# Output projection of a hybrid encoder layer: stores on another queue, loads issued two tiles ahead

## The chip, the core and the metric

The kernel runs on one core of a Trainium2 chip. TensorE (PE; PEld is its weight load) multiplies, VectorE (DVE), ScalarE (ACT) and GpSimd (POOL) do the rest, and SyncE (SP) and other engines issue DMA transfers between device memory and the on-chip buffers (SBUF; PSUM receives the matmuls). The metric is the device time of one execution in microseconds (us). SP's rows in the profile are DMA issues; a row with the engine name ACTq or POOLq is a DMA issued by that engine.

## The reference

One layer on 2048 tokens of width 1024, in float32. The normed input is projected; 8 heads of latent attention give 512 columns, a bidirectional S5 recurrence with GLU gives the other 512. Then, of the part that matters here:

```
mix = concat(rms_norm(attention) * g_a, rms_norm(s5) * g_s)     # 512 + 512 columns
h   = x + rms_norm(mix @ w_out) * g_post_mix                    # output projection
out = h + rms_norm(relu(rms_norm(h) @ w_up) ** 2 @ w_down) * g_post_mlp
```

## The kernel before, in words

The stages follow one another: input projection; attention head by head, with the S5 work in its gaps; the output projection, about 1583 to 1859 us of the profiled execution; the up projection of the MLP; the down projection. Each fp32 product is made of three matmuls of split halves (high and low part of each factor: `ah`/`al`, `sh`/`sl`, weights `woh`/`wol`).

Attention and S5 leave their results feature-major in DRAM: `AD` (attention, not yet divided by the softmax sums), `SD` (S5), and `RD2` (the reciprocals of the sums, two rows of heads per 128 features). The sums of the last head go to DRAM (`RD<-o`, L644), come back as `rr` (L647, GpSimd's queue), are inverted (L648) and stored (L649).

The output projection runs over 16 tiles of 128 tokens (`out_tile`). Per tile:

- `s_ops`: load `sr` from SD (L1116, one buffer), split into `sh`, `sl` (L125 on ScalarE, L126 on VectorE), square (L1109) and sum the blocks (`sq`, L1110).
- `a_ops`: load `ar` from AD (L1122, two buffers) and `rb` (L1126, two broadcast DMAs over 64 partitions each, one buffer), `ar` times `rb` on VectorE (L1128), then the same split, square and sum (`ah`, `al`, `aq`).
- `out_mm`: 24 matmuls on the S5 half and 24 on the attention half (`op`, L1182), into two PSUM banks each; two small products give the squared norms (`ss`), which VectorE copies to SBUF (`s2c`, L1203), and this frees their PSUM bank. GpSimd makes the two inverse norms (`rs_v`, `rs_r`, L131 and L132).
- ScalarE scales one half (`ot`, L1211), VectorE adds the other (`o`, L1212); ScalarE squares and sums (`jk`, L1216), VectorE scales by the norm and `gpo` (L1218) and adds the residual `xt` (L1219; loaded at L1196 in one buffer). `o` is stored to HD (L1220), squared once more (`jk`, L1225), and normed to `hn` (L1227).
- two tiles later (`hn_T`): 8 transposes (L1238), two copies to `hb` (L1243) and two stores to HTD (L1244), the feature-major input of the MLP.

Tile t is written with the attention factors of tile t+1 and the S5 factors of tile t+2 ahead of it. At tiles 10 and 11 a 1 MB load `traw` of HTD for the up projection is issued (L1273); from tile 9 on, factors of the first up weights (`raw`, `st`, L1264) are made between. All these DMAs but those of `rr` go through SP, in SP's program order: an issue that waits for a buffer or for a producer holds those behind it.

The order of each engine is not the program's: the Tile framework's scheduler places the instructions of each engine by a timeline model when the kernel is built, so a change in one place can move instructions elsewhere. PSUM has 8 banks, given out in turn.

Of the kernel before, what the change touches and what calls it, by code (L numbers as in the profile page):

```python
# [51 lines left out]
def hymba_layer_kernel(  # L52
# [75 lines left out]
    def rstd_of(ss, n, eps=EPS, rows=128):  # L128
        v = sm.tile([128, 1], F32, tag="rs_v", name="rs_v")
        r = sm.tile([128, 1], F32, tag="rs_r", name="rs_r")  # L130
        G.tensor_scalar(out=v[:rows], in0=ss, scalar1=1.0 / n, scalar2=eps, op0=ALU.mult, op1=ALU.add)  # L131
        G.tensor_tensor(out=r[:rows], in0=v[:rows], in1=mhalf[:rows], op=ALU.pow)  # L132
        return r
# [959 lines left out]
    def out_open():  # L1093
        ip = W["ip"] = ph.enter_context(pool("iO", 2, "right"))
        W["ep"] = ph.enter_context(pool("eO", 2, "right"))
        e1 = W["e1"] = ph.enter_context(pool("e1", 1, "right"))
        gpo = W["gpo"] = mk(e1, [128, D], "gpo")
        Y.dma_start(out=gpo, in_=g_post_mix[0].partition_broadcast(128))
        for t in range(2):
            W["s", t] = s_ops(t)  # L1100
            yield

    def halves(src, nm):
# [6 lines left out]
        V.reduce_sum(out=sq, in_=src.rearrange("p k c -> p c k"), axis=AX.X)  # L1110
        return h, l, sq

    def s_ops(t):
        cs = slice(t * 128, (t + 1) * 128)
        sr = W["ip"].tile([128, 4, 128], F32, tag="sr", name="sr", bufs=1)
        Y.dma_start(out=sr, in_=SD[:, cs].rearrange("(k p) c -> p k c", p=128))  # L1116
        return halves(sr, "s")

    def a_ops(t):
        cs = slice(t * 128, (t + 1) * 128)  # L1120
        ar = W["ip"].tile([128, 4, 128], F32, tag="ar", name="ar")
        Y.dma_start(out=ar, in_=AD[:, cs].rearrange("(k p) c -> p k c", p=128))  # L1122
        rb = W["ip"].tile([128, 4, 128], F32, tag="rb", name="rb", bufs=1)
        for b in range(2):
            src = RD2[b:b + 1, cs]
            Y.dma_start(out=rb[64 * b:64 * b + 64],  # L1126
                        in_=bass.AP(src.tensor, src.offset, [[0, 64], [2 * 2048, 4], [1, 128]]))
        V.tensor_tensor(out=ar, in0=ar, in1=rb, op=ALU.mult)  # L1128
        return halves(ar, "a")

# [57 lines left out]
        return sq, [out_mm(h, l, 4, half) for half in range(2)]  # L1188

    def out_tile(t, between):  # L1190
        if t + 1 < NT:
            W["a", t + 1] = a_ops(t + 1)
        if t + 2 < NT:
            W["s", t + 2] = s_ops(t + 2)
        xt = W["e1"].tile([128, D], F32, tag="xt", name="xt")
        Y.dma_start(out=xt, in_=xv[t // 8, t % 8])  # L1196
        sqs, ps = W.pop(("ps", t), None) or out_s(t)
        h, l, sqa = W.pop(("a", t))
        p = pa("ss")
        T.matmul(out=p[:, 0:2], lhsT=sqa, rhs=ones)  # L1200
        T.matmul(out=p[:, 2:4], lhsT=sqs, rhs=ones)
        s2 = sm.tile([128, 4], F32, tag="s2c", name="s2c")
        V.tensor_copy(s2, p[:, 0:4])  # L1203
        ra = rstd_of(s2[:, 0:1], 512)
        rb = rstd_of(s2[:, 2:3], 512, eps=4 * EPS)
        o = W["ep"].tile([128, D], F32, tag="o", name="o")
        for half in range(2):
            hs = slice(half * 512, (half + 1) * 512)
            p = out_mm(h, l, 0, half)
            tm = W["e1"].tile([128, 512], F32, tag="ot", name="ot")  # L1210
            S.activation(out=tm, in_=p, func=AF.Copy, scale=ra)  # L1211
            V.scalar_tensor_tensor(out=o[:, hs], in0=ps[half], scalar=rb, in1=tm, op0=ALU.mult, op1=ALU.add)  # L1212
        between()
        jk = W["e1"].tile([128, 512], F32, tag="ot", name="jk").bitcast(BF16)
        ss = sm.tile([128, 1], F32, tag="ss", name="ss")
        S.activation(out=jk, in_=o, func=AF.Square, accum_out=ss)  # L1216
        r = rstd_of(ss, D)
        V.scalar_tensor_tensor(out=o, in0=o, scalar=r, in1=W["gpo"], op0=ALU.mult, op1=ALU.mult)  # L1218
        V.tensor_tensor(out=o, in0=o, in1=xt, op=ALU.add)  # L1219
        Y.dma_start(out=HD[t], in_=o)  # L1220

        hn = wraw.tile([128, 8, 256], F32, tag="raw", name="raw")[:, 0:4].rearrange("p k c -> p (k c)") if t == NT - 1 else \
            W["e1"].tile([128, D], F32, tag="hn", name="hn", bufs=2)
        ss = sm.tile([128, 1], F32, tag="ss", name="ss")
        S.activation(out=jk, in_=o, func=AF.Square, accum_out=ss)  # L1225
        r = rstd_of(ss, D)
        V.scalar_tensor_tensor(out=hn, in0=o, scalar=r, in1=gpr, op0=ALU.mult, op1=ALU.mult)  # L1227
        return hn

    def hn_T(t, hn):  # L1230
# [10 lines left out]
        b = hn if t == NT - 1 else mk(tq, [128, D], "hb")  # L1241
        for a in range(2):
            S.copy(out=b[:, a * 512:(a + 1) * 512], in_=ps[a])  # L1243
            Y.dma_start(out=HTD[ct].rearrange("k p b c -> p k b c")[:, :, 2 * a + i // 4, cs],  # L1244
                        in_=b[:, a * 512:(a + 1) * 512].rearrange("p (k c) -> p k c", k=4))

    NP = FF // 256
# [23 lines left out]
    def s_load(ct, k):  # L1271
        RAW[ct, k] = raw = tst.tile([128, 4, 512], F32, tag="traw", name="traw")
        Y.dma_start(out=raw, in_=HTD[ct, k])  # L1273

    W["a", 0] = a_ops(0)
    for t in range(2):
        W["ps", t] = out_s(t)
# [291 lines left out]
```

## Time and profile before

| what | value |
|---|---|
| median of 3 runs | 3214.03 us (3213.02 to 3215.77) |
| the profiled execution, its own time | 3213.55 us |
| its span in the trace | 3211.7 us |
| mean granted TensorE clock | 0.973 |
| PE busy over the span | 3032.7 us, 94% |
| DVE, ACT, POOL busy | 1848.8, 1638.6, 1255.2 us |
| bytes on the hardware queue `q1` | 275.10 MB of 279.51 |
| output projection, first and last `s2c` | 1618.3 and 1835.6 us |

PE is busy 94% over the whole kernel, which says little of one stage. To read a stage, take the windows of time (how busy each engine is in it), then the waits in it (which engine waits, at which line, and for what), then the rows of one engine in order of time. A wait named "DMA ar<-AD" ends when that transfer has landed; the name of a tile stands without its buffer's number, so "RD" is `RD` or `RD2`.

### The profile page before, as it was taken

To read this page: it belongs to the slowest core of one execution; us is meant where nothing else is said; L and a number is where in the kernel's file an instruction comes from. 1 tells how busy PE (TensorE), PEld (TensorE's weight loads), DVE (VectorE), ACT (ScalarE), POOL (GpSimd) and SP (SyncE) were. 2 spreads that over 40 slices of the span, in tenths; PEclk is the share of its full clock that TensorE was granted. 3 is DMA by queue.
4 is the path that set the end of the run, shared out by engine and by line. 5 is a ranking of instruction groups with operands and counts; after the bars stand their busy time and mean duration, and the time that the engine had idled before them with its cause. 6 is when DMAs were issued, how large, how long until landed. Compare 5 with 4: busy or idle time off the path is not lost.

```text
span 3211.7 us, 42406 instructions
## 1 busy us (share of the span) xinstructions
PE 3032.7 (94%) x14455; PEld 2419.7 (75%) x14455; DVE 1848.8 (58%) x2893; ACT 1638.6 (51%) x3081; POOL 1255.2 (39%) x2363
## 2 busy tenths in 40 slices
PE   6999988989999999999879879999999999999998
PEld 6899956666777766678767658886888888888887
DVE  6333278767888876675356584448444234444447
ACT  4333356988777799974435445445445421111112
POOL 4222245775888876600032275447544000000002
PEclk8999989999999999999989989999999999999999
DMA  4232231211001022232246543333333422222215
GB/s 151 65 86 74 73 75 27 58 46 33 20 18 27 24 70 85 65 113 63 65 112 179 164 154 115 109 114 119 109 107 106 142 81 73 73 79 73 69 63 203
DMA packets 244377, 279.51 MB, mean 87 GB/s; under 512 B 35920, under 2 KB 180688, under 8 KB 243136
## 3 DMA queue, kind: packets, MB, share of 16 engines
q1 hardware_dynamic: 242112, 275.10, 28.1%
q8 instruction: 113, 1.85, 0.2%
q10 hardware_dynamic: 1792, 1.57, 0.2%
q14 instruction: 104, 0.85, 0.1%
q0 software_dynamic: 256, 0.14, 0.0%
HBM read 181.31 MB, written 95.36 MB: 86 GB/s over the span
## 4 chain that ended last, share of the span: by engine, by line
PE 57%; issue 6%; DVE 4%; ACT 4%; POOL 3%; DMA 2%; SPq 0%; POOLq 0%; DVEq 0%; ACTq 0%
PE dn L1514 20%; PE pE L1329 5%; PE pB L1329 5%; PE pA L1329 4%; PE s L619 3%; PE s L621 2%; PE s L620 2%; PE z L1079 2%; PE X L611 2%; PE pF L1329 2%; PE X L612 2%; PE X L613 2%; PE mxp L573 2%; POOL rs_r L132 1%; DMA rb<-RD 1%
## 5 line engine op out<-in xcount | busy, mean ns | idle before, releaser
L627 DVE TENSOR_TENSOR pl<-s,ph 128x512 fp32r<-128x512 f32 x512 | 350.2, 686 | 163.1 <-ACT s L626 157.0
L623 ACT ACTIVATE ph<-s 128x512 fp32r<-128x512 f32 (+1 forms) x544 | 323.4, 595 | 171.9 <-PE s L621 158.6
L1514 PE MATMUL dn<-dl,ah 128*128 128x512 f32 x1024 | 398.8, 389 | 0.0
L1514 PE MATMUL dn<-dh,ah 128*128 128x512 f32 x1024 | 398.8, 389 | 0.0
L1514 PE MATMUL dn<-dh,al 128*128 128x512 f32 x1024 | 398.7, 390 | 0.0
L574 DVE TENSOR_REDUCE mx<-mxp 128x1 f32<-128x512 f32 x512 | 343.0, 684 | 59.3 <-PE mxp L573 56.2
L125 ACT CAST ah<-mraw 128x512 fp32r<-128x512 f32 x128 | 79.5, 621 | 454.3 <-DMA mraw<-MD 273.8
L626 ACT ACTIVATE s<-s 128x512 f32<-128x512 f32 x512 | 304.1, 594 | 0.7
L1498 POOL TENSOR_TENSOR ss<-s2f 128x1 f32<-128x1 f32 x16 | 11.2, 699 | 702.2 <-ACT jk L1495 702.2
L1264 POOL TENSOR_TENSOR st<-raw 128x512 f32<-128x512 f32 x128 | 173.9, 1359 | 263.6 <-DVE al L126 263.5
L619 PE MATMUL s<-ql,kh 96*128 96x512 f32 (+1 forms) x544 | 226.9, 417 | 15.1 <-ACT ZS L937 4.9
L611 PE MATMUL X<-pl,vt 128*65 128x512 f32 x512 | 209.2, 409 | 29.8 <-DVE pl L627 27.9
L1519 DVE TENSOR_TENSOR acc<-dn,acc 128x512 f32<-128x512 f32 x224 | 153.0, 687 | 133.2 <-PE dn L1514 132.8
L1514 PEld LDWEIGHTS dn<-dl,ah 128*128 128x128 f32 x1024 | 192.4, 188 | 39.8
L1514 PEld LDWEIGHTS dn<-dh,al 128*128 128x128 f32 x1024 | 192.4, 188 | 39.7
L1514 PEld LDWEIGHTS dn<-dh,ah 128*128 128x128 f32 x1024 | 192.3, 188 | 39.7
L620 PE MATMUL s<-qh,kl 96*128 96x512 f32 (+1 forms) x544 | 218.3, 401 | 0.0
L621 PE MATMUL s<-qh,kh 97*128 97x512 f32 (+1 forms) x544 | 215.0, 401 | 0.7 <-DMA qh<-nm 0.7
L573 PE MATMUL mxp<-kh,qh 96*128 96x512 f32 x512 | 199.3, 411 | 13.2 <-DVE mx L574 5.2
L612 PE MATMUL X<-ph,vt 128*64 128x512 f32 x512 | 205.3, 401 | 0.0
L613 PE MATMUL X<-ph,vt 128*65 128x512 f32 x512 | 205.1, 401 | 0.0
L126 DVE TENSOR_TENSOR al<-mraw,ah 128x512 fp32r<-128x512 f32 x128 | 88.5, 691 | 197.8 <-ACT ah L125 188.2
(811 smaller groups left out, 7822.8 us busy)
## 6 DMA issues: line engine op xcount, KB each, us to landing
raw<-in_w_mlp_up_dram SPq DMA_DIRECT2D x32, 1024.0 KB
MD<-r SPq DMA_DIRECT2D x128, 256.0 KB
mraw<-MD SPq DMA_DIRECT2D x128, 256.0 KB
xt<-in_x_dram SPq DMA_DIRECT2D x32, 512.0 KB
raw<-in_w_mlp_down_dram SPq DMA_DIRECT2D x32, 512.0 KB
ug<-UD SPq DMA_DIRECT2D x32, 256.0 KB
HD<-o SPq DMA_DIRECT2D x16, 512.0 KB
traw<-HTD SPq DMA_DIRECT2D x8, 1024.0 KB
```

Of the source, the lines that this page charges most:

```text
L574: V.reduce_max(out=mxs[n][:, j, b:b + 1], in_=p, axis=AX.X)
L611: T.matmul(out=X[:65], lhsT=v[:, t, 0:65], rhs=pl_, start=(t == 0), stop=False)
L612: T.matmul(out=X[:64], lhsT=v[:, t, 65:129], rhs=ph_, start=False, stop=False)
L613: T.matmul(out=X[:65], lhsT=v[:, t, 0:65], rhs=ph_, start=False, stop=False)
L619: T.matmul(out=s[:m], lhsT=kh[0:96, cs], rhs=ql, start=True, stop=False)
L620: T.matmul(out=s[:m], lhsT=kl[:, cs], rhs=qh[0:96], start=False, stop=False)
L621: T.matmul(out=s[:m], lhsT=kh[:, cs], rhs=qh, start=False, stop=True)
L623: S.activation(out=ph_[:m], in_=s[:m], func=AF.Exp, scale=SCALE)
L626: S.activation(out=s, in_=s, func=AF.Exp, scale=SCALE)
L627: V.tensor_tensor(out=pl_, in0=s, in1=f(ph_), op=ALU.subtract)
L1329: T.matmul(out=p, lhsT=a[:, k], rhs=b, start=(first and k == 0 and j == 0), stop=(k == 3 and j == 2), skip_group_check=not first)
L1514: T.matmul(out=p, lhsT=a[:, ts_], rhs=c[:, hs], start=(q == 0 and w == 0), stop=(q == FB - 1 and w == 2))
```

## The change

In the output projection:

- The stores to HD (L1241 after) and HTD (L1260) are issued by ScalarE (`S.dma_start`) and no more by SP (`Y.dma_start`). HD stands behind the second `jk`.
- `loads(t)` issues `sr`, `xt`, `ar` and `rb` of a tile; `out_tile(t)` calls it for t+1 and t+2 at its head, so what isn't loaded yet is issued two tiles ahead.
- `sr`, `rb` have two buffers; `xt` moves to another pool (`tq`), also with two. `ar` had two and keeps them.
- The S5 factors of tile t+1 (they were those of t+2) are made in tile t.

```diff
--- before.py
+++ after.py
@@ -1097,6 +1097,7 @@
         gpo = W["gpo"] = mk(e1, [128, D], "gpo")
         Y.dma_start(out=gpo, in_=g_post_mix[0].partition_broadcast(128))
         for t in range(2):
+            sd_load(t)
             W["s", t] = s_ops(t)
             yield
 
@@ -1110,21 +1111,34 @@
         V.reduce_sum(out=sq, in_=src.rearrange("p k c -> p c k"), axis=AX.X)
         return h, l, sq
 
+    def sd_load(t):
+        cs = slice(t * 128, (t + 1) * 128)
+        W["sr", t] = sr = W["ip"].tile([128, 4, 128], F32, tag="sr", name="sr")
+        Y.dma_start(out=sr, in_=SD[:, cs].rearrange("(k p) c -> p k c", p=128))
+
     def s_ops(t):
-        cs = slice(t * 128, (t + 1) * 128)
-        sr = W["ip"].tile([128, 4, 128], F32, tag="sr", name="sr", bufs=1)
-        Y.dma_start(out=sr, in_=SD[:, cs].rearrange("(k p) c -> p k c", p=128))
-        return halves(sr, "s")
-
-    def a_ops(t):
+        return halves(W.pop(("sr", t)), "s")
+
+    def loads(t):
+
+        if ("x", t) in W:
+            return
+        if ("sr", t) not in W and t > 1:
+            sd_load(t)
+        W["x", t] = xt = tq.tile([128, D], F32, tag="xt", name="xt", bufs=2)
+        Y.dma_start(out=xt, in_=xv[t // 8, t % 8])
         cs = slice(t * 128, (t + 1) * 128)
         ar = W["ip"].tile([128, 4, 128], F32, tag="ar", name="ar")
         Y.dma_start(out=ar, in_=AD[:, cs].rearrange("(k p) c -> p k c", p=128))
-        rb = W["ip"].tile([128, 4, 128], F32, tag="rb", name="rb", bufs=1)
+        rb = W["ip"].tile([128, 4, 128], F32, tag="rb", name="rb")
+        W["ar", t] = ar, rb
         for b in range(2):
             src = RD2[b:b + 1, cs]
             Y.dma_start(out=rb[64 * b:64 * b + 64],
                         in_=bass.AP(src.tensor, src.offset, [[0, 64], [2 * 2048, 4], [1, 128]]))
+
+    def a_ops(t):
+        ar, rb = W.pop(("ar", t))
         V.tensor_tensor(out=ar, in0=ar, in1=rb, op=ALU.mult)
         return halves(ar, "a")
 
@@ -1188,12 +1202,14 @@
         return sq, [out_mm(h, l, 4, half) for half in range(2)]
 
     def out_tile(t, between):
+        for u in range(t + 1, t + 3):
+            if u < NT:
+                loads(u)
         if t + 1 < NT:
             W["a", t + 1] = a_ops(t + 1)
-        if t + 2 < NT:
-            W["s", t + 2] = s_ops(t + 2)
-        xt = W["e1"].tile([128, D], F32, tag="xt", name="xt")
-        Y.dma_start(out=xt, in_=xv[t // 8, t % 8])
+            if ("ps", t + 1) not in W:
+                W["s", t + 1] = s_ops(t + 1)
+        xt = W.pop(("x", t))
         sqs, ps = W.pop(("ps", t), None) or out_s(t)
         h, l, sqa = W.pop(("a", t))
         p = pa("ss")
@@ -1217,12 +1233,12 @@
         r = rstd_of(ss, D)
         V.scalar_tensor_tensor(out=o, in0=o, scalar=r, in1=W["gpo"], op0=ALU.mult, op1=ALU.mult)
         V.tensor_tensor(out=o, in0=o, in1=xt, op=ALU.add)
-        Y.dma_start(out=HD[t], in_=o)
 
         hn = wraw.tile([128, 8, 256], F32, tag="raw", name="raw")[:, 0:4].rearrange("p k c -> p (k c)") if t == NT - 1 else \
             W["e1"].tile([128, D], F32, tag="hn", name="hn", bufs=2)
         ss = sm.tile([128, 1], F32, tag="ss", name="ss")
         S.activation(out=jk, in_=o, func=AF.Square, accum_out=ss)
+        S.dma_start(out=HD[t], in_=o)
         r = rstd_of(ss, D)
         V.scalar_tensor_tensor(out=hn, in0=o, scalar=r, in1=gpr, op0=ALU.mult, op1=ALU.mult)
         return hn
@@ -1241,7 +1257,7 @@
         b = hn if t == NT - 1 else mk(tq, [128, D], "hb")
         for a in range(2):
             S.copy(out=b[:, a * 512:(a + 1) * 512], in_=ps[a])
-            Y.dma_start(out=HTD[ct].rearrange("k p b c -> p k b c")[:, :, 2 * a + i // 4, cs],
+            S.dma_start(out=HTD[ct].rearrange("k p b c -> p k b c")[:, :, 2 * a + i // 4, cs],
                         in_=b[:, a * 512:(a + 1) * 512].rearrange("p (k c) -> p k c", k=4))
 
     NP = FF // 256
@@ -1272,6 +1288,7 @@
         RAW[ct, k] = raw = tst.tile([128, 4, 512], F32, tag="traw", name="traw")
         Y.dma_start(out=raw, in_=HTD[ct, k])
 
+    loads(0)
     W["a", 0] = a_ops(0)
     for t in range(2):
         W["ps", t] = out_s(t)
```

How the instructions move, in the order in which each engine has them. First SP at the end of attention, with buffer numbers (`ar`, `rb`, `sr`, `xt` are the loads of the first tiles; `AD`, `RD` from `o` the stores of the last attention head). Before:

```order
L1196 DMA xt_19152<-in_x_dram 128x1024
L1126 DMA rb_19132<-RD2_78 64x4x128 x2
L1116 DMA sr_18936<-SD_76 128x4x128
L1122 DMA ar_19218<-AD_75 128x4x128
L1126 DMA rb_19220<-RD2_78 64x4x128 x2
L1126 DMA rb_19308<-RD2_78 64x4x128
L1116 DMA sr_19143<-SD_76 128x4x128
L1126 DMA rb_19308<-RD2_78 64x4x128
L1122 DMA ar_19306<-AD_75 128x4x128
L1126 DMA rb_19437<-RD2_78 64x4x128 x2
L643 DMA AD_75<-o_19038 64x512
L644 DMA RD_77<-o_19038 1x512
```

After:

```order
L1132 DMA ar_19134<-AD_75 128x4x128
L1137 DMA rb_19136<-RD2_78 64x4x128 x2
L1137 DMA rb_19145<-RD2_78 64x4x128 x2
L1117 DMA sr_19139<-SD_76 128x4x128
L1117 DMA sr_19220<-SD_76 128x4x128
L1137 DMA rb_19226<-RD2_78 64x4x128 x2
L1132 DMA ar_19143<-AD_75 128x4x128
L1132 DMA ar_19224<-AD_75 128x4x128
L1137 DMA rb_19314<-RD2_78 64x4x128 x2
L1137 DMA rb_19443<-RD2_78 64x4x128 x2
L643 DMA AD_75<-o_19038 64x512
L644 DMA RD_77<-o_19038 1x512
```

The `rb` pair of tile 5 (rb_19443) and the S5 load of tile 3 (sr_19220) now stand ahead of the `RD<-o` store, and tile 2's `rb` pair (rb_19145) comes directly behind tile 1's. In VectorE's order, the rows that end with the `s2c` of tile 2 (`al<-st`, `al<-raw`: factors of the up weights). Before:

```order
L126 TENSOR_TENSOR al<-ar,ah 128x512
L1219 TENSOR_TENSOR o<-o,xt 128x1024
L1110 TENSOR_REDUCE aq<-ar 128x128
L126 TENSOR_TENSOR al<-st,ah 128x512
L126 TENSOR_TENSOR al<-raw,ah 128x512
L126 TENSOR_TENSOR al<-st,ah 128x512
L1203 COPY s2c<-ss 128x4
L126 TENSOR_TENSOR sl<-sr,sh 128x512
L126 TENSOR_TENSOR al<-st,ah 128x512
L126 TENSOR_TENSOR al<-raw,ah 128x512
```

After:

```order
L1235 TENSOR_TENSOR o<-o,xt 128x1024
L126 TENSOR_TENSOR al<-ar,ah 128x512
L1111 TENSOR_REDUCE aq<-ar 128x128
L1142 TENSOR_TENSOR ar<-ar,rb 128x512
L126 TENSOR_TENSOR al<-raw,ah 128x512
L1219 COPY s2c<-ss 128x4
L126 TENSOR_TENSOR sl<-sr,sh 128x512
L1243 SCALAR_TENSOR_TENSOR hn<-o,rs_r,gpr 128x1024
L126 TENSOR_TENSOR al<-st,ah 128x512
```

Three `al` stood between the last `aq` and `s2c`; the `ar` product of a later tile and the `al` that stood further up stand there now, and those three behind.

SP at tiles 10 and 11, where the `traw` loads stand. Before:

```order
L1116 DMA sr<-SD 128x4x128
L1244 DMA HTD<-hb 128x4x128 x2
L1273 DMA traw<-HTD 128x2048 x2
L1122 DMA ar<-AD 128x4x128
L1220 DMA HD<-o 128x1024
L1196 DMA xt<-in_x_dram 128x1024
L1116 DMA sr<-SD 128x4x128
L1126 DMA rb<-RD_78 64x4x128
```

After:

```order
L1137 DMA rb<-RD_78 64x4x128 x2
L1117 DMA sr<-SD 128x4x128
L1289 DMA traw<-HTD 128x2048
L1132 DMA ar<-AD 128x4x128
L1289 DMA traw<-HTD 128x2048
L1129 DMA xt<-in_x_dram 128x1024
L1117 DMA sr<-SD 128x4x128
L1137 DMA rb<-RD_78 64x4x128 x2
```

The HTD and HD stores are gone from the row, and one `traw` stands ahead of the `ar` load instead of two.

ScalarE in the middle of the stage, one tile. Before:

```order
L1211 ACTIVATE ot<-op,rs_r 128x512 x2
L125 CAST ah<-ar 128x512
L1243 COPY hb<-hT 128x512 x2
L1216 ACTIVATE jk,ss<-o 128x1024
L1109 ACTIVATE ar<-ar 128x512
L125 CAST sh<-sr 128x512
L1225 ACTIVATE jk,ss<-o 128x1024
L1109 ACTIVATE sr<-sr 128x512
```

After:

```order
L1227 ACTIVATE ot<-op,rs_r 128x512 x2
L125 CAST ah<-ar 128x512
L1259 COPY hb<-hT 128x512 x2
L1232 ACTIVATE jk,ss<-o 128x1024
L1260 DMA HTD<-hb 128x4x128 x2
L1110 ACTIVATE ar<-ar 128x512
L125 CAST sh<-sr 128x512
L1240 ACTIVATE jk,ss<-o 128x1024
L1241 DMA HD<-o 128x1024
L1110 ACTIVATE sr<-sr 128x512
```

The HTD pair stands between the first `jk` and the square of `ar`, the HD store between the second `jk` and the square of `sr`; the computing instructions keep their order.

## The prediction

> **What bounds the kernel now.** First the list of waits, 1570 to 1840 us (engine, line, what it waited for: us in total, times, longest). The output projection is the only part that the change touches.
>
> ```profile
> DVE ar L1128 <- DMA ar<-AD: 24.8, 11, 6.4
> ACT sh L125 <- DMA sr<-SD: 24.8, 5, 10.7
> PE op L1182 <- DVE s2c L1203: 18.8, 6, 7.6
> DVE ar L1128 <- DMA rb<-RD: 17.2, 3, 7.3
> DVE ar L1128 <- DMA HD<-o: 5.9, 1, 5.9
> SPq L1244 <- ACT hb L1243: 49.5, 16, 7.4
> SPq L1126 <- DVE ar L1128: 22.6, 6, 7.5
> SPq L1122 <- DVE aq L1110: 20.9, 11, 2.6
> SPq L1273 <- DMA HTD<-hb: 5.7, 1, 5.7
> ```
>
> PE's `op` matmuls wait for `s2c`, the small copy that frees a PSUM bank; VectorE reaches `s2c` late, because `ar·rb` (L1128), which stands ahead of it, waits for a load. No row has VectorE waiting for `xt`. How much is at stake comes from stretches of time (window, its length, busy us and instructions of PE, PEld, DVE, ACT, POOL, then granted clock, DMA share, GB/s):
>
> ```profile
> 1763.00:1800.00 37.00, 28.55 (x123) 22.84 (x122) 18.38 (x23) 14.61 (x27) 6.81 (x18) 0.86 0.64 199
> 1800.00:1841.30 41.30, 41.30 (x201) 34.37 (x201) 25.03 (x29) 18.45 (x33) 14.02 (x29) 1.00 0.45 140
> 1618.00:1622.00 4.00, 4.00 (x21) 3.34 (x21) 0.44 (x2) 0.00 (x0) 0.00 (x0) 1.00 0.29 43
> 1624.00:1628.00 4.00, 0.63 (x3) 0.55 (x4) 0.00 (x0) 1.21 (x2) 1.50 (x4) 1.00 1.01 352
> ```
>
> From 1800 on PE never stops: 201 matmuls in 41.3 us. A tile has 60 (48 `op`, 8 transposes, and 4 for `ss`), so its floor is 60 × 41.3 / 201 = 12.3 us. The `s2c` of a tile marks its pace; those of tiles 0, 2, 5, 6, 10, 11 and 12, and the VectorE rows ahead of them (start, duration, in brackets the idle time before and what ended it):
>
> ```profile
> 1618.31 0.16 DVE L1203 COPY s2c<-ss 128x4 f32<-128x4 f32 x1
> 1629.38 0.35 DVE L648 RECIPROCAL rr<-rr 128x32 f32<-128x32 f32 x1 [10.91 <-DMA rr<-RD]
> 1631.33 0.75 DVE L1212 SCALAR_TENSOR_TENSOR o<-op,rs_r,ot 128x512 f32<-128x512 f32 x1 [1.06 <-POOL rs_r L132]
> 1638.30 1.68 DVE L1128 TENSOR_TENSOR ar<-ar,rb 128x512 f32<-128x512 f32 x1 [0.54 <-DMA ar<-AD]
> 1644.81 0.68 DVE L126 TENSOR_TENSOR al<-st,ah 128x512 fp32r<-128x512 f32 x1
> 1647.69 0.15 DVE L1203 COPY s2c<-ss 128x4 f32<-128x4 f32 x1
> 1664.45 0.69 DVE L1128 TENSOR_TENSOR ar<-ar,rb 128x512 f32<-128x512 f32 x1 [3.47 <-DMA ar<-AD]
> 1680.49 0.69 DVE L1128 TENSOR_TENSOR ar<-ar,rb 128x512 f32<-128x512 f32 x1 [2.89 <-DMA ar<-AD]
> 1695.33 0.69 DVE L1128 TENSOR_TENSOR ar<-ar,rb 128x512 f32<-128x512 f32 x1 [0.44 <-DMA ar<-AD]
> 1695.94 0.15 DVE L1203 COPY s2c<-ss 128x4 f32<-128x4 f32 x1
> 1704.13 1.07 DVE L1110 TENSOR_REDUCE aq<-ar 128x128 f32<-128x512 f32 x1 [1.70 <-ACT ar L1109]
> 1709.75 0.69 DVE L1128 TENSOR_TENSOR ar<-ar,rb 128x512 f32<-128x512 f32 x1 [2.09 <-DMA ar<-AD]
> 1710.36 0.15 DVE L1203 COPY s2c<-ss 128x4 f32<-128x4 f32 x1
> 1762.23 0.15 DVE L1203 COPY s2c<-ss 128x4 f32<-128x4 f32 x1
> 1773.51 0.69 DVE L1128 TENSOR_TENSOR ar<-ar,rb 128x512 f32<-128x512 f32 x1 [5.92 <-DMA HD<-o]
> 1785.16 0.69 DVE L1128 TENSOR_TENSOR ar<-ar,rb 128x512 f32<-128x512 f32 x1 [5.03 <-DMA ar<-AD]
> 1785.77 0.15 DVE L1203 COPY s2c<-ss 128x4 f32<-128x4 f32 x1
> 1798.51 0.16 DVE L1203 COPY s2c<-ss 128x4 f32<-128x4 f32 x1 [0.28 <-PE ss L1201]
> ```
>
> Over the floor: tiles 0 to 5, 77.6 − 61.5 = 16.1 us; tiles 5 to 10, 66.3 − 61.5 = 4.8; tiles 10 to 12, where the 1 MB `traw` loads start, 36.3 − 24.6 = 11.7. Together 32.6 us, the most that better loads can give here.
>
> Why loads are late: one queue carries everything. While only an `rb` pair runs it moves 43 GB/s, so its 262 KB take 6.1 us; other traffic runs at 352. Per tile `ar`, `sr`, `xt`, HD and HTD are 2.1 MB, 6.0 us. In one FIFO that is 12.1 of the 13.3 us that tiles 5 to 10 take each: almost full.
>
> **The change, part by part.** *Stores on ScalarE's queue.* HD and HTD (1.05 MB, 3.0 us) leave the FIFO: 9.1 us a tile stay on SP's, and a load no longer stands behind a store that waits for its producer (the 49.5 us row). Does issuing cost ScalarE? HTD comes behind the `jk` of L1232, its `hb` written two ScalarE instructions earlier; HD behind the `jk` of L1240, which already waits for the same `o`. So neither adds a wait for data. The issue itself, from the stage where ScalarE already issues (a group and two rows), a `jk`, and the dearest HD and HTD issues of SP in this stage:
>
> ```profile
> L442 ACTq DMA_DIRECT2D QD<-qo x16: 310/311/362, 395.6 to 431.5; - x16
> 415.14 0.31 ACTq L442 DMA_DIRECT2D QD<-qo  x1
> 415.20 0.36 ACT L438 COPY qo<-qup 64x256 f32<-64x256 f32 x1
> 1702.40 1.08 ACT L1216 ACTIVATE jk<-o 128x1024 bf16<-128x1024 f32 x1
> 1764.83 0.75 SPq L1220 DMA_DIRECT2D HD<-o  x1
> 1805.80 1.88 SPq L1244 DMA_DIRECT2D HTD<-hb  x2
> ```
>
> A ScalarE issue took 0.31 us and the next copy began 0.06 us after its start, so it runs beside the work of the engine. The 1.08 us of `jk` ahead of each store can cover it likewise. Bounds: 0, and three issues × 0.31 = 0.9 us a tile where the cover is gone (14 tiles, 13 us). Behind the HTD pair stands `ar`², then `aq`, then the next `ar` load. I take 1 us in all, nearest to the rows that overlap.
>
> *Double-buffered `rb`.* Removes SP's 22.6 us of waits for L1128. *`sr` and `xt` doubled and early, S5 factors one tile ahead:* 0. Nothing waits for `xt`; the `sr` waits lie on ScalarE while `ot` has to wait for POOL's `rs_r` anyway. If that cover goes, `sh` and `sl` (a split like `al`, 0.68 us each half by that row) come late on PE's path: 1.4 us a tile. *`ar` stays at two buffers:* its load still starts only after `aq` two tiles back (the 20.9 us row). So `ar` isn't really two tiles ahead; what it gains is a shorter queue.
>
> *Head, tiles 0 to 5.* SP's rows where attention ends, and, for the part after, the `ar` load inside the steady loop:
>
> ```profile
> 1615.93 1.24 SPq L1126 DMA_DIRECT2D rb<-RD  x2
> ...
> 1705.23 0.36 SPq L1122 DMA_DIRECT2D ar<-AD  x1
> ```
>
> By the order of instructions the `rb` pair of tile 5 is put ahead of the `RD<-o` store on whose way back `rr` waits, and with it two pairs, 12.2 us, instead of one. They wait for the products of tiles 2 and 3 to free their buffers; the second buffer lets the pairs of these tiles follow each other without the wait for a product between, which I take to spare about one pair's 6.1 us ahead of 1615.93. Start 6.1 earlier and last 6.1 longer: the store lands when it does now. `o` of tile 0 then comes directly behind `rr`, and POOL makes both `rs_r` ahead of the `RD` store: 1629.38 + 0.35 = 1629.7 against 1631.33, gain 1.6. Three `al` of the up projection (1644.81 to 1647.69, 2.9 us) move behind the `s2c` of tile 2, and 0.5 of waiting goes: 5.0. They cost 2.9 in tile 3, where the wait of 3.47 goes: 5.6. Then the waits of 2.89 and 0.44: 8.9. Bounds: the extra pair could hold the store up by its whole 6.1 us, 1.6 − 6.1 = −4.5; at most 16.1. I take 8.9, because each piece has its row.
>
> *Tiles 5 to 10.* The loop runs from the end of `aq` (1705.2) over the `ar` load, issued at 1705.23 and waited for until 1709.75, 4.5 us, though 0.26 MB need 0.75 at 352 GB/s. The rest is queue. Of 4.8 us over the floor I take 3. Bounds 0.9 × 5 = −4.5 (issue cost in the loop), and 4.8.
>
> *`traw`, tiles 10 to 12.* Two 1 MB loads are issued ahead of `ar` of tile 12 (3.0 us each), and the first waits for an HTD store in the same FIFO. Now one is ahead of it, and the stores are elsewhere. A wait of at most 11.7 / 3 ≈ 4 stays: I take 8, bounds 2 (both transfers still share the bytes) and 11.7.
>
> The Trainium skill speaks to both sides, in "DMA: Bandwidth & Descriptors". Under "Queues, rings and completion order" every issuing row has its own ring per DMA engine, and an engine takes turns between rows packet by packet: by that a load no longer waits for a store in front. No row here shows it, since q1 carries nearly all of this kernel's bytes.
>
> *Sum:* 8.9 + 3 + 8 − 1 = 18.9 us. The profiled execution took 3213.55 us (its span 3211.7, 1.85 around it), 0.5 under the median of the runs shown: 3194.7, say 3195 us. The stages behind follow in a chain (their start is bound by VectorE and weights), and shift with it.
>
> **The rivals.** *No relief.* The same 16 engines carry the same bytes, and `ar`, with two buffers, is tied to `aq` as before. Then only 1.6 in the head and 3 at `traw` stay, less 1: 3.6, 3210 us, within what can't be told from none. For: 1.01 of DMA share at 352 GB/s, engines full in bursts. Against: 0.45 to 0.64 mean share, so queueing is mostly order, not bytes. The skill's section "Issuing engines are not separate DMA queues" on the same page says this outright: DMAs of several engines run on the same 16 and interleave, and all that one saves is sequencer time.
>
> *Slower: ScalarE blocked by issuing.* If the HTD pair costs ScalarE what its worst one cost SP (1.88) and HD its worst (0.75), that is 2.6 us in the `jk` to `ar`² to `aq` loop, × 14 tiles = 37, less the 18.9 + 1: +17, 3231 us. It decides from 19.9 / 14 = 1.4 us a tile. For: `hb` is written across 128 partitions in strided 512-element pieces, and the loop has no slack until 1800. Against: 0.06 us between issue and next start above.
>
> *All of it.* Loads always in time: 32.6 us less, 3181. For: PE at its floor from 1800 on with the same order. Against: `ar`'s two buffers.
>
> **How the numbers follow.** Forecast 0.55 (its own range 3185 to 3205), all of it 0.13, no relief 0.18, slower 0.14. 0.2%, 6.4 us, is about what a measurement here can tell from no change. Faster: 0.55 + 0.13 + 0.02 of no relief = 0.70; same 0.16; slower 0.14. The range 3180 to 3212 takes in no relief and nearly all of the fast end, and leaves out slower and a few hundredths.
>
> **What would show it.** Right: no VectorE wait for `ar<-AD` over 2 us between tiles 3 and 10; `s2c` of tile 2 about 5 us earlier; tiles 10 to 12 in under 29 us; HTD and HD rows as ACTq with ScalarE instructions starting beside them. Wrong: ScalarE idle gaps of an us behind each HTD pair (slower); the same `ar` waits with the stores elsewhere (no relief); `rr` later than 1629.4 (head). A new wait of PE for `sl` or `sh` would show that one tile ahead is too late for the S5 factors.

## The result, and the profile after

The changed kernel took 3196.59 us (median of 4 runs, 3194.03 to 3198.40) against 3214.90 (4 runs, 3213.02 to 3219.51): ratio 0.994, 95% interval 0.9923 to 0.9958. Faster by 0.6%, and 1.6 us from the forecast of 3195. The terms behind that forecast did not come out as they were put, so the closeness is luck. The profiled execution took 3196.28 us, with a span of 3194.5.

From the page of the changed kernel, first the queues (packets, MB, share of the 16 engines):

```profile
q1 hardware_dynamic: 222912, 258.32, 27.1%
q10 hardware_dynamic: 20992, 18.35, 1.7%
```

The stores are on a queue of their own now, 16.8 MB more on q10 than before. Then VectorE's rows in order of time: `rr`, the product `ar·rb` (L1142 now) where it waited, and `s2c` (L1219) of tiles 0, 2, 5, 10 and 12:

```profile
1614.58 0.16 DVE L1219 COPY s2c<-ss 128x4 f32<-128x4 f32 x1 [5.83 <-PE ss L1217]
1619.93 0.35 DVE L648 RECIPROCAL rr<-rr 128x32 f32<-128x32 f32 x1 [3.62 <-DMA rr<-RD]
1632.50 0.15 DVE L1219 COPY s2c<-ss 128x4 f32<-128x4 f32 x1
1665.65 0.69 DVE L1142 TENSOR_TENSOR ar<-ar,rb 128x512 f32<-128x512 f32 x1 [3.39 <-DMA ar<-AD]
1681.65 0.15 DVE L1219 COPY s2c<-ss 128x4 f32<-128x4 f32 x1
1695.70 0.69 DVE L1142 TENSOR_TENSOR ar<-ar,rb 128x512 f32<-128x512 f32 x1 [2.34 <-DMA ar<-AD]
1749.95 0.16 DVE L1219 COPY s2c<-ss 128x4 f32<-128x4 f32 x1
1758.42 0.69 DVE L1142 TENSOR_TENSOR ar<-ar,rb 128x512 f32<-128x512 f32 x1 [4.32 <-DMA ar<-AD]
1783.42 0.15 DVE L1219 COPY s2c<-ss 128x4 f32<-128x4 f32 x1
```

Set against the rows of before, the `s2c` of tile 2 comes 15.2 us earlier (1647.69), of tile 5 14.3 (1695.94), of tile 10 12.3 (1762.23), of tile 12 15.1 (1798.51); the span is 17.2 shorter. But the two traces don't run level. The store of the attention head before the last is issued ahead of every `sr`, `ar`, `rb` and `xt` load, and stands, before and then in the changed kernel, at

```profile
1556.98 0.50 SPq L643 DMA_DIRECT2D AD<-o  x1
1559.63 0.50 SPq L643 DMA_DIRECT2D AD<-o  x1
```

The changed kernel's trace is 2.7 us late there (1.6 to 2.9 us at the stores of this line from 478 us on), and so the change itself won 2.7 us more than those differences say: 17.8 by tile 2, 16.9 by tile 5. Then tiles 5 to 10 lose 2.0 (68.3 us instead of 66.3), and the `traw` tiles win 2.8 back. The waits for `ar` on VectorE, which the change was to shorten, are still there. In the list of waits, 1570 to 1840 us:

```profile
DVE ar L1142 <- DMA ar<-AD: 24.0, 10, 7.0
PE hT L1254 <- DVE hn L1243: 13.0, 9, 8.0
PE op L1196 <- DVE s2c L1219: 2.2, 3, 1.0
```

24.0 us in 10 waits, where before it was 24.8 in 11. PE's wait of its `op` matmuls for `s2c` fell to 2.2 (18.8 before), but its transposes now wait 13.0 for `hn`, where it was 2.3.

Where the 17 us in the head come from is seen in the rows of four engines there. In the kernel before: VectorE's product of tile 3, ScalarE's square of an S5 input and behind it its copy of the last attention result, SP's two stores of it, GpSimd's `rr` load (which waits until the sums have landed, though its bracket here names an `rb` transfer), and ScalarE's split of tile 3's S5 input with the first `ot` behind it:

```profile
1615.21 0.69 DVE L1128 TENSOR_TENSOR ar<-ar,rb 128x512 f32<-128x512 f32 x1 [6.38 <-DMA ar<-AD]
1616.54 0.63 ACT L1109 ACTIVATE sr<-sr 128x512 f32<-128x512 f32 x1 [3.53 <-DVE sl L126]
1617.19 0.58 ACT L641 COPY o<-X 65x512 f32<-65x512 f32 x1
1617.80 0.48 SPq L643 DMA_DIRECT2D AD<-o  x1
1618.33 0.44 SPq L644 DMA_DIRECT2D RD<-o  x1
1624.11 0.59 POOL L647 DMA_DIRECT2D rr<-RD  x1 [60.78 <-DMA rb<-RD]
1626.11 0.62 ACT L125 CAST sh<-sr 128x512 fp32r<-128x512 f32 x1 [8.34 <-DMA sr<-SD]
1626.63 0.68 ACT L1211 ACTIVATE ot<-op,rs_r 128x512 f32<-128x512 f32 x1
```

In the changed kernel:

```profile
1606.14 2.63 SPq L1137 DMA_DIRECT2D rb<-RD  x4
1606.63 0.68 DVE L1142 TENSOR_TENSOR ar<-ar,rb 128x512 f32<-128x512 f32 x1
1611.94 0.58 ACT L641 COPY o<-X 65x512 f32<-65x512 f32 x1 [2.53 <-PE X L608]
1612.55 0.48 SPq L643 DMA_DIRECT2D AD<-o  x1
1613.08 0.44 SPq L644 DMA_DIRECT2D RD<-o  x1
1615.71 0.60 POOL L647 DMA_DIRECT2D rr<-RD  x1 [49.52 <-DMA RD<-o]
1617.52 0.69 ACT L1227 ACTIVATE ot<-op,rs_r 128x512 f32<-128x512 f32 x1 [0.54 <-PE op L1196]
```

Before, the product of tile 3 waited for its `ar` until 1615.2. VectorE's `sl` came behind that product, ScalarE's square waited 3.5 us for `sl`, the copy stood behind the square, and so the stores of that result went out only at 1617.8. Now the product is done at 1607.3, the copy waits for nothing but PE's result, the sums store is issued 5.3 us earlier and lands 2.6 instead of 5.8 us after its issue: 8.4 us earlier in all by the traces' clocks, 11.1 with the 2.7 us. (Two `rb` pairs, of tiles 4 and 5, go ahead of it, in the row at 1606.14, but were all issued 4.3 us before it; in the kernel before one pair was issued only 1.2 us before it.) GpSimd and VectorE (`rr`) follow, and the first `ot` comes 9.1 us earlier; before, a load of `sr` stood in its way as well.

The theory to be tested: SP stood in the head behind the single `rb` buffer, and the loads behind it came late (theory Q in the expectations). The rival: it is the stores' queue (theory S).

### The profile page after: what moved, and what is told of

Same layout as the page of the kernel before. It is cut to its first block, busy times and chain, and to the rows that moved or that the text cites. A ratio compares the mean times of both kernels' runs of the same rounds, so it can differ in the third digit from the quotient of the medians.

```text
span 3194.5 us, 42377 instructions
## 1 busy us (share of the span) xinstructions
PE 3029.6 (95%) x14455; PEld 2416.3 (76%) x14455; DVE 1843.5 (58%) x2893; ACT 1640.0 (51%) x3081; POOL 1258.2 (39%) x2363
## 4 chain that ended last, share of the span: by engine, by line
PE 58%; issue 5%; DVE 4%; ACT 4%; DMA 2%; POOL 2%; SPq 0%; POOLq 0%; DVEq 0%; ACTq 0%
PE dn L1531 20%; PE pB L1346 5%; PE pE L1346 5%; PE pA L1346 5%; PE s L619 3%; PE s L621 2%; PE pF L1346 2%; PE s L620 2%; PE z L1079 2%; PE X L611 2%; PE X L612 2%; PE X L613 2%; PE mxp L573 2%; POOL rs_r L132 1%; ACT zh L125 1%
## 5 line engine op out<-in xcount | busy, mean ns | idle before, releaser
L611 PE MATMUL X<-pl,vt 128*65 128x512 f32 x512 | 208.8, 408 | 26.3 <-DVE pl L627 24.6
```

The lines of the kernel that those rows point to most:

```text
L611: T.matmul(out=X[:65], lhsT=v[:, t, 0:65], rhs=pl_, start=(t == 0), stop=False)
```

## The experiments

Lengths are differences of `s2c` starts in one profiled execution each, from the rows of that trace; the floor by the prediction's 12.3 us a tile is 36.9, 61.5 and 24.6 for the columns 2→5, 5→10 and 10→12. "Late" is how far the trace is behind that of before at the store shown above (1556.98 us there); take it off `rr at` to compare two rows. The stage of one execution can differ by several us from that of another: the profiled one of two `rb` is 6 us under its own median. All ratios are against the kernel before on the same chip. Last column: 95% interval of the ratio.

| kernel | median us (runs) | late | rr at | s2c 0→2 | 2→5 | 5→10 | 10→12 | ratio |
|---|---|---|---|---|---|---|---|---|
| before | 3214.9 (4) | 0 | 1629.4 | 29.4 | 48.2 | 66.3 | 36.3 | |
| the change | 3196.6 (4) | 2.7 | 1619.9 | 17.9 | 49.2 | 68.3 | 33.5 | 0.9923 to 0.9958 |
| two `rb` | 3208.8 (10) | −0.9 | 1622.3 | 26.0 | 48.8 | 65.2 | 34.2 | 0.9973 to 0.9991 |
| two `rb`, two `sr` | 3195.7 (4) | −0.2 | 1618.3 | 24.5 | 46.3 | 66.5 | 35.1 | 0.9926 to 0.9960 |
| ScalarE stores alone | 3229.7 (4) | 3.2 | 1633.1 | 29.6 | 48.2 | 78.0 | 33.7 | 1.0034 to 1.0064 |
| same, order restored | 3213.6 (10) | −1.4 | 1628.0 | 29.5 | 48.8 | 69.9 | 31.2 | 0.9994 to 1.0013 |
| change, stores on SP | 3198.4 (4) | 5.9 | 1621.1 | 18.6 | 51.7 | 66.7 | 35.7 | 0.9940 to 0.9970 |
| change, one `rb` | 3212.2 (10) | 1.2 | 1629.8 | 27.2 | 51.7 | 69.0 | 34.7 | 0.9985 to 1.0004 |
| change, three `ar` | 3199.8 (4) | 2.1 | 1626.7 | 28.6 | 48.2 | 69.2 | 27.4 | 0.9946 to 0.9976 |
| change, order | 3189.1 (4) | 3.6 | 1618.8 | 18.0 | 46.9 | 65.7 | 33.2 | 0.9903 to 0.9936 |
| three `ar` and order | 3185.5 (4) | 1.2 | 1626.0 | 28.5 | 39.2 | 63.8 | 25.9 | 0.9901 to 0.9931 |
| same, store first | 3187.9 (4) | 0.1 | 1619.5 | 33.4 | 39.2 | 64.3 | 26.7 | 0.9902 to 0.9932 |
| same, tile 6 behind xt 0 | 3183.9 (4) | 0.3 | 1623.5 | 24.1 | 44.4 | 62.0 | 26.1 | 0.9892 to 0.9926 |
| same, tile 6 behind xt 1 | 3182.7 (4) | 0.5 | 1622.3 | 25.8 | 39.4 | 63.9 | 26.3 | 0.9886 to 0.9919 |

(Tile 0's `s2c` isn't at the same place of the work in each, so `rr` and the sum of the columns say more than the first column alone.)

**Two rb buffers in the kernel before**

```diff
-        rb = W["ip"].tile([128, 4, 128], F32, tag="rb", name="rb", bufs=1)
+        rb = W["ip"].tile([128, 4, 128], F32, tag="rb", name="rb")
```

> The kernel before with one edit: rb has two buffers; stores, xt, sr and the order of the factors as before. Theory Q (SP held in the head): in the kernel before, the rb load of tile 3 waited on SP for the product of tile 2, held the ar load of tile 3 behind it, and with it the product, the square of sr, the copy of the last attention result and its two stores; two rb buffers alone should bring the AD store from 1617.8 to about 1613. The S5 load of tile 3 is still issued behind these stores, and ScalarE's split of it stands ahead of ot of tile 0, so not all of the 14.3 us of tiles 0 to 5 come: 5 to 11 us, 3203 to 3209 us. Theory S (the stores' queue makes the gain): nothing moves, 3211 to 3215, AD store later than 1616.

Measured: 3208.82 us, 5 faster, at the edge of the range. Its ten runs lie between 3202.85 and 3210.65, and the profiled one is the fastest, so its lengths flatter it. The sums store was issued at 1613.52 and `rr`'s load at 1616.17, as Q said. On ScalarE in that head:

```profile
1612.38 0.58 ACT L641 COPY o<-X 65x512 f32<-65x512 f32 x1
1617.68 0.62 ACT L125 CAST sh<-sr 128x512 fp32r<-128x512 f32 x1 [4.72 <-DMA sr<-SD]
1618.21 0.68 ACT L1211 ACTIVATE ot<-op,rs_r 128x512 f32<-128x512 f32 x1
```

The copy is at 1612.4 (1617.19 before), but then ScalarE waits 4.7 us for the S5 load of tile 3, which is still issued behind the stores, and `ot` stands behind that. The copy itself now stands behind the split of the S5 load before that one, which ScalarE waited for as well.

**Two rb and two sr buffers in the kernel before**

```diff
-        sr = W["ip"].tile([128, 4, 128], F32, tag="sr", name="sr", bufs=1)
+        sr = W["ip"].tile([128, 4, 128], F32, tag="sr", name="sr")
-        rb = W["ip"].tile([128, 4, 128], F32, tag="rb", name="rb", bufs=1)
+        rb = W["ip"].tile([128, 4, 128], F32, tag="rb", name="rb")
-        xt = W["e1"].tile([128, D], F32, tag="xt", name="xt")
+        xt = tq.tile([128, D], F32, tag="xt", name="xt")
```

> As the run before, with two buffers for sr also, and xt (still one buffer) taken from the pool tq so that it fits. Stores stay on SP, S5 factors two tiles ahead. SP's order up to the last attention stores is then that of the changed kernel. Theory Q: s2c of tile 2 at 1633 to 1636 (changed kernel 1632.5, before 1647.7), rr near 1620, and the traw stage as before: 3199 to 3204 us. If it is the stores' queue (theory S): 3209 or more, and rr near 1629.

Measured: 3195.65, 3 us under theory Q's range and the whole gain of the change, with the stores on SP, `ar`, `rb` and `xt` issued as in the kernel before, and the S5 factors still two tiles ahead. The second `sr` buffer is worth 13 us on top of the second `rb` buffer (3208.82 to 3195.65). ScalarE's first `ot` there:

```profile
1609.20 0.62 ACT L125 CAST sh<-sr 128x512 fp32r<-128x512 f32 x1 [1.46 <-PE op L1182]
1611.74 0.63 ACT L1109 ACTIVATE sr<-sr 128x512 f32<-128x512 f32 x1 [1.92 <-DVE sl L126]
1613.06 0.69 ACT L1211 ACTIVATE ot<-op,rs_r 128x512 f32<-128x512 f32 x1 [0.69 <-POOL rs_r L132]
```

`ot` at 1613.1, where it was 1626.63 before and 1618.2 in the run above: the split ahead of it waits for no load any more. (`xt` moved pools with it, to make room; that part was not tried apart, nor a second `sr` buffer without the second `rb` in the kernel before.)

**The stores alone on ScalarE**

```diff
-        Y.dma_start(out=HD[t], in_=o)
+        S.dma_start(out=HD[t], in_=o)
-            Y.dma_start(out=HTD[ct].rearrange("k p b c -> p k b c")[:, :, 2 * a + i // 4, cs],
+            S.dma_start(out=HTD[ct].rearrange("k p b c -> p k b c")[:, :, 2 * a + i // 4, cs],
```

> The kernel before with one edit: the HD and HTD stores are issued by ScalarE; all loads and buffers as before. Theory Q: the head has no store of this stage in it, so rr stays at 1629 within 1 us and s2c of tile 2 near 1647; the traw stage gains 2 to 8 us; tiles 5 to 10 change by under 2: 3206 to 3212 us. Theory S: 10 us or more, under 3204.

Both theories missed: 3229.65, slower by 15.5 us. The head is as before (`rr` 1633.1, in a trace that was 3.2 us late before the stage began); tiles 5 to 10 take 78.0 us instead of 66.3. The issues are not long: 0.34 us for HD and 0.37 to 0.70 for HTD in the tiles around 1715 to 1748 us. VectorE's rows tell it:

```profile
1725.00 1.28 DVE L1218 SCALAR_TENSOR_TENSOR o<-o,rs_r,gpo 128x1024 f32<-128x1024 f32 x1 [0.88 <-POOL rs_r L132]
1729.17 0.69 DVE L1128 TENSOR_TENSOR ar<-ar,rb 128x512 f32<-128x512 f32 x1 [2.89 <-DMA ar<-AD]
1729.78 1.22 DVE L1219 TENSOR_TENSOR o<-o,xt 128x1024 f32<-128x1024 f32 x1
1730.92 0.16 DVE L1203 COPY s2c<-ss 128x4 f32<-128x4 f32 x1
```

In this kernel the scheduler put the addition `o + xt` (L1219) behind the product that waits for a load; in the kernel before it stands ahead of it from tile 5 on. So the addition, `s2c` and what follows wait with the product.

**The same with VectorE's order restored**

```diff
-        V.tensor_tensor(out=ar, in0=ar, in1=rb, op=ALU.mult)
+        with tc.issue_after(W["oadd", t - 5]) if t >= 8 else ExitStack():
+            V.tensor_tensor(out=ar, in0=ar, in1=rb, op=ALU.mult)
-        V.tensor_tensor(out=o, in0=o, in1=xt, op=ALU.add)
+        W["oadd", t] = V.tensor_tensor(out=o, in0=o, in1=xt, op=ALU.add).ins
```

`issue_after` puts an instruction behind another in its engine's order, without a wait.

> As the run with the stores alone on ScalarE, with one edit: from tile 8 on VectorE issues the product ar times rb of a tile behind the addition of xt of the tile five before it, which is the order that the kernel before has there; ScalarE's order and the queues stay. Theory O (the scheduler's new order made that run slow: the addition stood behind the wait for the ar load): tiles 5 to 10 come back from 78.0 us to 66 to 70, and the time to 3216 to 3222 us. Theory A (ScalarE's issuing is what costs): tiles 5 to 10 stay above 75 and the time above 3225.

Measured: 3213.59, a bit faster than theory O's range and no different from the kernel before; tiles 5 to 10 take 69.9. The addition no longer waits:

```profile
1718.51 1.22 DVE L1220 TENSOR_TENSOR o<-o,xt 128x1024 f32<-128x1024 f32 x1
1721.42 0.70 DVE L1129 TENSOR_TENSOR ar<-ar,rb 128x512 f32<-128x512 f32 x1 [1.69 <-DMA ar<-AD]
1722.05 0.15 DVE L1204 COPY s2c<-ss 128x4 f32<-128x4 f32 x1
```

So the 15 us were the order and not ScalarE's issuing. And the stores' queue by itself brings nothing that shows in the time: here tiles 5 to 10 are 3.6 us longer than before and tiles 10 to 12 5.1 shorter.

**The change with the stores back on SP**

```diff
-        S.dma_start(out=HD[t], in_=o)
+        Y.dma_start(out=HD[t], in_=o)
-            S.dma_start(out=HTD[ct].rearrange("k p b c -> p k b c")[:, :, 2 * a + i // 4, cs],
+            Y.dma_start(out=HTD[ct].rearrange("k p b c -> p k b c")[:, :, 2 * a + i // 4, cs],
```

> The changed kernel with one edit: HD and HTD stores back on SP's queue. Theory Q: rr near 1620 and s2c of tile 2 near 1632.5 as in the changed kernel; tiles 5 to 10 within 2 us of its 68.3; tiles 10 to 12 longer by 2 to 6 us than its 33.5; 3198 to 3204 us. Theory S: all of the gain goes, 3210 to 3216.

3198.37 us, as Q expected: 1.8 us above the change, and the two intervals overlap. Tiles 2 to 5 are 2.6 us longer, tiles 10 to 12 2.2, tiles 5 to 10 1.6 shorter, in a profiled execution that is 4.7 us above its own median. So in the changed kernel a gain of a few us by the stores' queue is neither shown nor excluded; the head's gain doesn't need it.

**The change with one rb buffer**

```diff
-        rb = W["ip"].tile([128, 4, 128], F32, tag="rb", name="rb")
+        rb = W["ip"].tile([128, 4, 128], F32, tag="rb", name="rb", bufs=1)
```

> The changed kernel with one edit: rb has one buffer again; loads still issued ahead, sr and xt doubled, stores on ScalarE. Theory Q (two rb buffers let SP go on in the head): the ar load of tile 3 is late again, the AD store near 1617, rr at 1625 to 1630, and 8 us or more of the gain are lost: 3205 to 3212 us. If sr's second buffer alone is what counts: 3198 or less.

3212.24, just above Q's range: all of the gain is gone, with everything else of the change in place. SP's rows there, four `rb` issues that last 9.85 us together and the stores late again:

```profile
1607.62 9.85 SPq L1137 DMA_DIRECT2D rb<-RD  x4
1618.12 0.48 SPq L643 DMA_DIRECT2D AD<-o  x1
1618.64 0.44 SPq L644 DMA_DIRECT2D RD<-o  x1
```

With the two runs with two `rb` in the kernel before this settles the head: neither buffer alone brings it, `rb`'s second is necessary, and both together (with `xt` in its other pool) are enough.

**Three ar buffers**

```diff
-        W["x", t] = xt = tq.tile([128, D], F32, tag="xt", name="xt", bufs=2)
+        W["x", t] = xt = tq.tile([128, D], F32, tag="xt", name="xt")
-        ar = W["ip"].tile([128, 4, 128], F32, tag="ar", name="ar")
+        ar = W["ip"].tile([128, 4, 128], F32, tag="ar", name="ar", bufs=3)
```

> The changed kernel with ar in three buffers; xt has one, to make room. Theory L (in tiles 5 to 12 s2c waits, by VectorE's order, for an ar load that could only start after aq two tiles earlier): no wait for ar<-AD is left between tiles 5 and 10, these take 61.5 to 64 us (68.3 in the changed kernel), tiles 10 to 12 under 30 (33.5); 3180 to 3190 us. Rival: the loads are late by the queues' load and not by the buffers: the waits stay, 3194 to 3199.

Theory L failed as it was put: 3199.80, just above its rival's range, tiles 5 to 10 69.2, with waits as before:

```profile
1704.62 0.69 DVE L1142 TENSOR_TENSOR ar<-ar,rb 128x512 f32<-128x512 f32 x1 [1.87 <-DMA ar<-AD]
1705.23 0.15 DVE L1219 COPY s2c<-ss 128x4 f32<-128x4 f32 x1
```

The count of products ahead of each `s2c` shows why. In the changed kernel the product right before the `s2c` of tile 6 is that of tile 9, three tiles ahead, though `s2c` needs nothing of it. Given a third buffer, the scheduler put the product of tile 10 there, four ahead, so that it waits for a load again. The third buffer was spent on running further ahead. (Tiles 10 to 12 did gain: 27.4 us instead of 33.5.) In the head one more `rb` pair, tile 6's, and the `ar` load of tile 4 went ahead of the sums store: it took 5.5 us to land, and `rr` came at 1626.7.

**Three ar buffers and the order**

```diff
-        V.tensor_tensor(out=ar, in0=ar, in1=rb, op=ALU.mult)
+        with tc.issue_after(W["oadd", t - 5]) if t >= 6 else ExitStack():
+            V.tensor_tensor(out=ar, in0=ar, in1=rb, op=ALU.mult)
```

(with `W["oadd", t]` the addition of `xt`, as above)

> As the run with ar in three buffers, and from tile 6 on the product ar times rb is issued behind the addition of xt of the tile five before, so that this addition never stands behind a load. Theory L and O: tiles 2 to 5, where the changed kernel has the other order, get 2 to 5 us shorter (49.2 there); 3177 to 3188 us, not slower than the run with three buffers alone. Rival: the order makes no difference once the loads are early: within 2 us of that run.

3185.50, within the range, and 14 us less than three buffers alone. Ahead of tile 6's `s2c` stands tile 9's product again, but its load had a whole tile more, and after the head no product waits for one. The same place as in the fence above:

```profile
1692.37 1.23 DVE L1236 TENSOR_TENSOR o<-o,xt 128x1024 f32<-128x1024 f32 x1
1693.51 0.69 DVE L1143 TENSOR_TENSOR ar<-ar,rb 128x512 f32<-128x512 f32 x1
1694.11 0.15 DVE L1220 COPY s2c<-ss 128x4 f32<-128x4 f32 x1
```

Tiles 2 to 5 take 39.2 us (49.2 in the change), 5 to 10 63.8, 10 to 12 25.9: near the floor in all three. Only the head is worse than in the change, and by tile 5, with the lateness taken off, the two are within 1.1 us.

**The order alone**, in the changed kernel with its two `ar` buffers, by the same edit:

> The changed kernel (two ar buffers) with the order alone: from tile 6 on the product ar times rb issues behind the addition of xt of the tile five before it. If order is most of the 14 us that order and third buffer gave together over the third buffer alone: 3186 to 3193 us. If it needs the third buffer, since the load can't start before aq: 3194 to 3199 us, with waits for ar<-AD of 1 to 4 us as in the changed kernel.

3189.08, on the side of the order, though its interval touches that of the change. Tiles 2 to 5 are 2.2 us shorter, 5 to 10 2.6; some of the waits for `ar` stay (0.4 to 4.9 us). The `traw` tiles need the third buffer: 33.2 us here, 25.9 with it.

**The head of that version.** Three tries to have its store and `rr` as early as in the change:

```diff
-        Y.dma_start(out=RD[h:h + 1, cs], in_=o[64:65])
+        W["rdst"] = Y.dma_start(out=RD[h:h + 1, cs], in_=o[64:65]).ins
     def loads(t):
         if ("x", t) in W:
             return
+        with tc.issue_after(W["rdst"]) if t >= 4 else ExitStack():
+            loads_(t)
+
+    def loads_(t):
```

> The run with three ar buffers and the order, with one edit: SP issues the loads of tiles 4 and up behind the last attention head's sums store, so that no rb pair of theirs stands ahead of it. Theory: in that run the store was issued at 1614.7 and its data came back into GpSimd's hands only at 1620.5, 5.9 us later, behind three rb pairs; without them it takes under 3.5 us as in the changed kernel (2.6), rr comes before 1622, tiles 0 to 2 take under 22 us (28.5): 3174 to 3181 us. Rival: the store's way is not what bounds the head there (ar loads late), or the loads that are put behind are missed later: 3183 or more.

3187.87, no gain. The store landed 2.3 us after its issue, but the `rb` pairs now behind it were ahead of other things:

```profile
1611.44 0.59 POOL L647 DMA_DIRECT2D rr<-RD  x1 [47.95 <-DVE s2c L1224]
1619.51 0.35 DVE L648 RECIPROCAL rr<-rr 128x32 f32<-128x32 f32 x1 [6.71 <-DMA rr<-RD]
1633.15 1.23 DVE L1240 TENSOR_TENSOR o<-o,xt 128x1024 f32<-128x1024 f32 x1 [6.34 <-DMA xt<-in_x_dram]
```

`rr`'s 16 KB, on GpSimd's queue, took 8.1 us, and `xt` of tile 0 came 6.3 us late. The expected rival.

```diff
+        with tc.issue_after(W["xdma", 0]) if t >= 6 else ExitStack():
+            loads_(t)
```

(in place of the one above, with `W["xdma", t]` the `xt` load of tile t)

> The run with three ar buffers and the order, with one edit: SP issues the loads of tiles 6 and up behind the xt load of tile 0, so the rb pairs of tiles 4 and 5 go ahead of the sums store as in the changed kernel, that of tile 6 behind it and behind xt. Theory (the head loses by rb pairs wherever they stand ahead of what is needed next): store to GpSimd's hands under 4 us (5.9 in the run with three buffers and the order), xt in time, tiles 0 to 2 under 24 us (28.5): 3174 to 3182 us. Rival: two pairs ahead of the store hold it as three did: 3184 to 3188.

3183.86, 2 us over the theory's range and just under the rival's. The store landed in 2.4 us, as the theory said, and `xt` was in time; `rr`'s load took 6.0 us.

```diff
-        with tc.issue_after(W["xdma", 0]) if t >= 6 else ExitStack():
+        with tc.issue_after(W["xdma", 1]) if t >= 6 else ExitStack():
```

> As the run before it (loads of tiles 6 and up behind the xt load of tile 0), but behind the xt load of tile 1. In that run the sums came back fast (2.4 us), and then the load of rr on GpSimd's queue took 6.0 us beside tile 6's rb pair (4.2 in the changed kernel). Theory: transfers of other queues slow it, since they use the same engines; with the pair gone rr's load takes under 4.6 us, rr is 1.5 to 3 us earlier against the store than there, and the time 3178 to 3183 us. Rival: rr's load is slowed by gpr and xt, which stay: 6 us again, 3182 to 3187.

3182.65, which both ranges hold, but the theory's reason fell: with no `rb` pair beside it `rr`'s load still took 6.3 us, the rival's number.

```profile
1615.66 0.38 SPq L1274 DMA_DIRECT2D raw<-in_w_mlp_up_dram  x1
```

By this row the 1 MB `raw` load of the up weights was issued 0.3 us ahead of `rr`'s (1615.96); in the change it came 3.4 us behind it. Over all runs it goes with what SP issues around it. It took 2.8 us in two of them, the change with the stores on SP and the order alone, where SP's next load was issued 0.4 us behind it, 4.2 in the change, where that came at the same time, and 5 to 8 us in all others, where loads were issued ahead of it, by 0.3 to 5.5 us. Which of the loads counts, and why, stays open, since no run moves one of them alone. The four versions with order and three buffers can't be told apart by their intervals; the last, 0.9886 to 0.9919, beats both the kernel before and the change (0.9923 to 0.9958).

## Why the prediction was right, and where it was not

The time was right by luck: a term too small and two too large cancelled. At tile 12's `s2c`, with the 2.7 us of lateness taken off, 8.9 + 3 + 8 − 1 = 18.9 had become 16.9 − 2.0 + 2.8 = 17.7.

- **Head, 8.9 put, 16.9 measured, beyond its bound of 16.1.** The step that failed: "Start 6.1 earlier and last 6.1 longer: the store lands when it does now." It landed 8.4 us earlier by the traces' clocks, 11.1 with the lateness taken off. The rate of the `rb` pairs was right (42 to 43 GB/s again in the changed trace from 1608 to 1612 us), but the two pairs were issued 9.8 us earlier than the one pair before, not 6.1, and didn't hold the store up for the time of a second pair. The path to the store's issue was left out: SP's wait for the single `rb` buffer held `ar` of tile 3, and by VectorE and ScalarE the copy of the result that is stored. The 22.6 us row of SP's waits for L1128 was quoted, and priced by its own queue only, not by what stood behind it on three engines. Of the 16.9 us, 6.4 lie ahead of tile 0's `s2c`, which the sum took as fixed; from there to tile 5 it is 10.6.
- **sr at 0: wrong.** The cover named for its wait, that `ot` has to wait for `rs_r` anyway, was itself moved by the other edit. With `rb` alone doubled ScalarE's wait for the S5 load stands ahead of `ot`, and the second buffer is worth 13 us.
- **Three al behind s2c of tile 2:** they moved as the order says. With the waits that were to go, tiles 2 to 5 were put 3.9 us shorter, and are 0.9 longer (49.2, 48.2 before). The wait of 3.47 ahead of tile 3's `s2c` did go, but one of 3.4 (1665.65) now stands ahead of tile 4's, where 2.89 stood.
- **Tiles 5 to 10, 3 put, −2.0 measured.** The step that failed is that the rest of the 4.5 us from issue to product is queue. With the stores gone the `ar` load took 4.8 us from the issue to the product at 1695.70 (3.4 to 4.8 over these tiles, 2.8 to 4.6 before), no less:

```profile
1690.94 0.37 SPq L1132 DMA_DIRECT2D ar<-AD  x1
```

 The bound of −4.5 held it. The loop was seen rightly as tied to `aq` by two buffers, but not that VectorE's order is what makes `s2c` wait for a product three tiles ahead of it. Order with a third buffer shows that, and the order alone points the same way.
- **traw, 8 put, 2.8 measured.** One load ahead instead of two leaves waits of 4.3 and 1.5 us; with a third `ar` buffer the same tiles take 6 to 8 us less. The buffer was the term, the queue the smaller part.
- **ScalarE's issue, 1 put:** borne out as small, by the restored order; in the change one HTD issue took 1.69 us and delayed `ar`² by 0.72:

```profile
1744.12 1.69 ACTq L1260 DMA_DIRECT2D HTD<-hb  x1
1745.85 0.63 ACT L1110 ACTIVATE ar<-ar 128x512 f32<-128x512 f32 x1 [0.72 <-issue]
```

- **xt early, S5 factors one tile ahead:** 0, and no run shows a gain or a cost: without both, two more buffers give 3195.65. The wait of PE for `sl` or `sh` that would have spoken against it isn't in PE's list of waits.
- **The rivals.** "No relief" was wrong in its time, 3210, since it put the head at 1.6, but right for the stores' queue, which gives nothing that shows: 3198.37 with and 3196.59 without SP's stores, 3213.59 against 3212.97 in the kernel before. The Trainium skill's "Issuing engines are not separate DMA queues" ("DMA: Bandwidth & Descriptors") agrees with that. The rule under "Queues, rings and completion order" on the same page of the Trainium skill, by which an engine takes turns between the rings, may hold too, but no run here shows a gain by it. "Slower" came true in its time for the stores alone (3229.65, 1.4 us from its price), by chance and by another mechanism: not ScalarE's issues, but the order in which the scheduler then put VectorE's instructions. (Its price took 1.88 us as the dearest HTD pair of SP; the trace of before has one of 2.48 at 1655.10.)

## What to carry to other kernels

A second buffer is worth what stands behind the wait on the issuing queue, not what that wait costs its own tile: follow each issue that stands behind it to the engine that needs it. Where a scheduler sets the order, a change of a queue or of a buffer count is also a change of order: look at what stands ahead of the instruction that frees the next resource, and tie that order down before a buffer is added. When two waits cover each other, price both at the sum of removing them together, not each at zero.

## What was not expected

- Moving stores between queues made the kernel 15.5 us slower by the scheduler's order alone, and one ordering edge gave all of it back.
- A third `ar` buffer without an order edge gave nothing in tiles 5 to 10 (69.2 us, 68.3 in the change); the edge then took 14 us off the whole.
- A load of 16 KB (`rr`) on a queue of its own took from 2.8 to 8.1 us from issue to use, according to whether SP's loads were issued ahead of it or behind.
